# A decoder's recurrence on one core: TensorE's order written out over four head pairs, the triangular solve moved to GpSimd, and a plain fp32 start

## The chip, the cores and the metric

The kernel runs on one core of one Trainium2 chip. The metric is the device time of one execution in microseconds; lower is better. Three runs of the kernel before gave 2741.23, 2740.06 and 2737.32 us, so the time before is their median, 2740.06 us. A profiled execution gives the trace that is read below.

## The reference

The model is a trunk of two layers over 272 positions (16 meta tokens and 256 tokens) with 2048 channels: an RWKV-7 layer with a gated FFN, then a stick-breaking attention layer with another. The change touches only the first part, the RWKV-7 mixing and the norm ahead of it. Cut to what matters:

```python
hn = rms_norm(h, mix_norm_g[0])                     # over 2048 channels
xx = token_shift(hn) - hn
xr, xw, xk, xv, xa, xg = (hn + xx * mu[i] for i in range(6))
r, k, v = xr @ w_r, xk @ w_k, xv @ w_v              # 2048 x 2048 each
decay = exp(-exp(-softplus(-(dec_w0 + tanh(xw @ dec_w1) @ dec_w2)) - 0.5))
a = sigmoid(a_w0 + (xa @ a_w1) @ a_w2)
g = sigmoid(xg @ g_w1) @ g_w2
kk = normalise_per_head(k * k_k)                    # 32 heads of 64
k = k * (1 + (a - 1) * k_a)
# for every head, position by position:
sa = state @ -kk_t
state = state * d_t + outer(sa, kk_t * a_t) + outer(v_t, k_t)
y_t = state @ r_t
y = group_norm(y) * gn_w + gn_b
bonus = sum(r * k * r_k, per head) * v
h = h + ((y + bonus) * g) @ w_o
```

## The kernel before

Activations lie transposed: channels on the 128 partitions, 272 positions along the free dimension, 16 tiles for 2048 channels. A projection makes one block of 128 output channels from 16 k-tiles. To hold precision at speed, each weight tile and each activation is split into a high and a low part (ACT casts, DVE subtracts, L172/L173 for weights, L254/L255 for activations), and a k-tile is three matmuls (`mm3k`, L191 to L193). Weights come as raw tiles of 1024 columns, eight k-tiles, into three buffers (`raw`) over SyncE's queue, and the split parts go to six buffers of four k-tiles.

**Prologue** (L374 on). RMS norm, the shifted mixes, all 16 blocks of w_k, and the hidden layers of the small products dec_w1, a_w1 and g_w1. The first three w_k blocks are split ahead in `presplit` and run together, k-tile by k-tile, as the activations get ready; `key_out` adds each finished block's squares into the key norm `kq` (L469).

**Scan.** Sixteen pairs of heads; one call of the generator `pair` does one pair. The recurrence is computed in chunks: 16 meta positions, then four chunks of 64. In order of the code a pair goes through: LoRA products `zw`, `za` with their decay terms P and pe; the projections of v and r (32 k-tiles); score products `ba`, `bb`, masked into `G` (L721); the bonus sum (L727, `blk` in fp32) and `z0`; the triangular solve; `tb`, `tv`, `kv`; two doubling rounds `yb`, `zb` (the transpose `Tn`, L827, reads the solved blocks `Tt`); apply `wa` to `Ah`; trans `rm` to `Rh` and `Mp`; states and four steps into `cb` (L896, L903); group norm `vb` (L916), gate `gp`, and the output `o`.

The solve inverts 40 small triangles of 16 by 16. G and SC0 are written to DRAM (`s1`), read back with one triangle on each of 40 partitions (`As`), solved by one DVE instruction and 14 pairs of a multiply and an add (L772, L777, L779), written back (`s2`) and read into `Tt`. These transfers go by ACT's queue (L754, L756, L760, L780, L783).

`interleave` starts a pair every 13 ticks and advances all that run by a yield each; the scheduler then decides each engine's order. When all pairs have their fronts, `wo_head` begins the first four w_o blocks with 15 of 16 k-tiles, and `wo_first` finishes them and does the others.

After the scan come the first FFN, the attention and the second FFN, which the change leaves alone.

Of the kernel before, what the change touches and what calls it, by code (L numbers as in the profile page):

```python
# [40 lines left out]
L2B = {"da": 1, "g": 2}  # L41
# [3 lines left out]
NSQ = 4  # L45
RSTEP = 7
KR = 8
FRONT = {"zw", "za", "vc", "bonus", "ba", "bb", "z0", "k0", "b00", "b01"}
TAIL = {"wa", "rm0", "rm1", "cb", "vb", "gp"}
WAIT1 = 3  # L50
WAIT2 = 9
STRIDE = 13
PSTEP = 8
NHEAD = 4
KHEAD = 15
ASTRIDE = 2
ASTEP = 4
BUFS = {n: 2 for n in "ARV BK AR0 bv G An Tt pe X BV0 WV0".split()}


def _consts():
# [14 lines left out]
    put("blk", blk)  # L76
    put("blk64", blk / 64)
# [6 lines left out]
    put("mask3", np.concatenate([incl, strict, incl], 1))  # L84
# [20 lines left out]
    first = pos  # L105
    put("onesD", np.full((128, 128), 1.0 / D))
# [17 lines left out]
class Builder:  # L124
# [141 lines left out]
    def build(self):  # L266
        tc, nc = self.tc, self.nc
        with ExitStack() as ctx:
# [6 lines left out]
            nc.scalar.dma_start(self.vecs, self.a["vecs"])  # L275
            self.dvec = {"hdw0": 0, "ha0": NK, "oka": 2 * NK}
            self.dvec.update({f"om{i}": (3 + i) * NK for i in range(6)})
            self.dv = cp.tile([128, 9 * NK + 4], F32, name="dv")
            b = 9 * NK
            nc.vector.memset(self.dv[:, b:b + 1], RMS_EPS)  # L280
            nc.vector.memset(self.dv[:, b + 1:b + 2], GN_EPS)
            nc.vector.memset(self.dv[:, b + 2:b + 3], 1.0)
            self.eps = self.dv[:, b:b + 1]
            self.gneps = self.dv[:, b + 1:b + 2]
            self.one = self.dv[:, b + 2:b + 3]

            def v16(name):
                i = VEC.index(name) * NK
                return self.vecs[:, i:i + NK]

            for dst, src in (("hdw0", "dec_w0"), ("ha0", "a_w0")):
                o = self.dvec[dst]
                nc.vector.tensor_scalar(self.dv[:, o:o + NK], v16(src), 0.5, None, ALU.mult)
            nc.vector.tensor_scalar(self.dv[:, 2 * NK:3 * NK], v16("k_a"), -1.0, 1.0,
                                    ALU.mult, ALU.add)
            nc.vector.tensor_scalar(self.dv[:, 3 * NK:9 * NK], self.vecs[:, 0:6 * NK], -1.0, 1.0,
                                    ALU.mult, ALU.add)
            nv = len(VEC) * NK
            self.kgain = self.vecs[:, nv:nv + 1]
            self.qgain = self.dv[:, b + 3:b + 4]  # L300
            nc.vector.tensor_scalar(self.qgain, self.vecs[:, nv + 1:nv + 2], 128.0 ** -0.5, None,
                                    ALU.mult)
# [34 lines left out]

    def time_mix(self):
# [4 lines left out]
        self.xs2 = self.hid_ctx.enter_context(tc.tile_pool(name="xs2", bufs=2 * NK))  # L343
        self.kp = self.hid_ctx.enter_context(tc.tile_pool(name="kp", bufs=NK))
# [5 lines left out]
        self.fronts = 0  # L350
        with ExitStack() as ctx:
            sp = ctx.enter_context(tc.tile_pool(name="sp", bufs=1))
            self.l2 = ctx.enter_context(tc.tile_pool(name="l2", bufs=2))
            self.dq = nc.scalar
            self.static = []
            self.s2 = []
            zero = sp.tile([128, 5, 65], F32, name="zero", tag="P")
            nc.gpsimd.memset(zero, 0.0)
            for i in range(2):
                st = {}  # L360
                for n, w in (("B0", 64), ("V0", 64), ("SC0", 128)):
# [5 lines left out]
                                  zero.rearrange("p a t -> p (a t)"))  # L367
                self.s2.append(z)
            self.interleave(lambda p: self.pair(p, sp), STRIDE, self.wo_head())
# [4 lines left out]
    def prologue(self, hid):  # L374
# [3 lines left out]
        with ExitStack() as ctx:  # L378
# [3 lines left out]
            hn = [self.xs2.tile([128, T + 1], F32, name="hn", tag="s") for _ in range(NK)]  # L382
            xx = [self.xs2.tile([128, T], F32, name="xx", tag="s") for _ in range(NK)]
            for k in range(NK):
                nc.sync.dma_start(xx[k], a["xT"][:, k, :])
# [14 lines left out]
            rstd = self.rstd_of(ss[:, :T])  # L400


            w0 = [[] for _ in range(G0)]
            raws = []
            n = 0

            def presplit(k0):
                nonlocal raws, n
                if k0 % 8 == 0:
                    raws = []  # L410
                    for m in range(G0):
                        raw = self.wraw.tile([128, 1024], F32, name="raw", tag="raw")
                        nc.sync.dma_start(raw, a["w_k"][m][:, k0 * 128:k0 * 128 + 1024])
                        raws.append(raw)
                for m in range(G0):
                    pool, t = (wx, ("w", "w")) if n < NWX // 2 else (self.whl, ("whi", "wlo"))
                    hi = pool.tile([128, 512], F32R, name="whi", tag=t[0])
                    lo = pool.tile([128, 512], F32R, name="wlo", tag=t[1])
                    n += 1
                    part = raws[m][:, k0 % 8 * 128:k0 % 8 * 128 + 512]  # L420
                    A.copy(hi, part)
                    V.tensor_tensor(lo, part, hi.bitcast(F32), ALU.subtract)
                    for k in range(4):
                        w0[m].append((hi[:, k * 128:k * 128 + 128], lo[:, k * 128:k * 128 + 128]))
# [155 lines left out]
    def pair(self, p, sp):  # L580

        nc, a = self.nc, self.a
        V = nc.vector
# [612 lines left out]
```

## Time and profile before

| | us |
|---|---|
| median of three runs | 2740.06 |
| the profiled execution | 2741.77 |
| span of its trace | 2740.0 |
| first key sum (prologue's first three blocks done) | 53.4 |
| last key sum | 173.1 |
| first mask G of pair 0, last of pair 15 | 194.5, 629.7 |
| first sum of h after w_o | 686.5 |

So the prologue takes some 190 us, the scan some 490 us, and the three stages after it the other 2050 us. A row of the trace's timeline begins with start and duration in us, then engine, line, operation, destination<-source; a group's row ends with busy time, mean duration in ns and what the engine waited for just before. A bracket holds the idle time ahead of an instruction and what ended it. "PE" is TensorE, "PEld" its weight loads, "DVE" VectorE, "ACT" ScalarE, "POOL" GpSimd, "SP" SyncE, and a "q" behind the name its queue of DMA issues. The chain of waits is the chain of work that ended last, followed back.

### The profile page before, as it was taken

How to read it: one execution, taken by the hardware profiler on the slowest of the kernel's cores; microseconds unless marked ns; L12 is line 12 of the kernel's file. 1: busy time of each engine (PE TensorE's matmuls, PEld its weight loads, DVE VectorE, ACT ScalarE, POOL GpSimd, SP SyncE). 2: the span in 40 equal slices, each digit the busy share in tenths (PEclk: the TensorE clock that was granted, in tenths of full speed). 3: DMA queues.
4: the chain of work that ended last, by engine and by line, in shares of the span. 5: the costliest groups of instructions: out<-in, count | busy, mean ns of one | idle time of the engine just before them, and what ended most of it. 6: DMA issues, size and time to landing. Idle time of an engine off the chain costs nothing.

```text
span 2740.0 us, 53870 instructions
## 1 busy us (share of the span) xinstructions
PE 2689.3 (98%) x20862; PEld 2475.0 (90%) x20862; DVE 1864.8 (68%) x4176; ACT 1493.5 (55%) x3005; POOL 1.2 (0%) x11
## 2 busy tenths in 40 slices
PE   6999999998999999999999999999999999999999
PEld 5888888887999999999999999988888888888888
DVE  7677788786666555555556876577776666666665
ACT  6774555555554444444445764477555455454553
POOL 0000000000000000000000000000000000000000
PEclk9999999999999999999999999999999999999999
DMA  5443333332655555555555555533555665665655
GB/s 169 135 152 100 104 96 103 104 95 83 210 173 168 181 177 167 185 176 162 187 176 167 180 164 169 169 119 105 189 187 179 196 188 180 197 189 179 199 177 179
DMA packets 181279, 439.50 MB, mean 160 GB/s; under 512 B 57984, under 2 KB 84000, under 8 KB 181024
## 3 DMA queue, kind: packets, MB, share of 16 engines
q1 hardware_dynamic: 137632, 428.56, 49.4%
q10 hardware_dynamic: 43392, 7.52, 1.5%
q8 instruction: 163, 2.67, 0.4%
q14 instruction: 92, 0.75, 0.1%
HBM read 430.27 MB, written 5.74 MB: 159 GB/s over the span
## 4 chain that ended last, share of the span: by engine, by line
PE 91%; DVE 3%; DMA 3%; ACT 2%; ACTq 1%; issue 0%; SPq 0%; DVEq 0%
PE mm L197 22%; PE mm L191 16%; PE mm L193 16%; PE mm L192 15%; PE mm L196 11%; DMA raw<-w_k 1%; PE cb L903 1%; PE yb L831 1%; PE rm L871 1%; PE zb L848 1%; PE hms L1038 1%; PE cb L896 1%; PE z L1115 1%; DVE G L721 0%; PE ba L715 0%
## 5 line engine op out<-in xcount | busy, mean ns | idle before, releaser
L173 DVE TENSOR_TENSOR wlo<-raw,whi 128x512 fp32r<-128x512 f32 (+1 forms) x1596 | 1079.0, 679 | 622.3 <-ACT whi L172 598.7
L172 ACT CAST whi<-raw 128x512 fp32r<-128x512 f32 (+1 forms) x1596 | 967.6, 611 | 906.2 <-PE mm L192 577.0
L191 PE MATMUL mm<-hl,whi 128*128 128x272 f32 x3424 | 996.9, 292 | 19.4 <-ACT hl L254 18.5
L193 PE MATMUL mm<-hl,wlo 128*128 128x272 f32 x3424 | 995.9, 291 | 0.0
L192 PE MATMUL mm<-hl,whi 128*128 128x272 f32 x3424 | 991.4, 290 | 0.4 <-DVE hl L255 0.3
L197 PE MATMUL mm<-hl,whi 128*128 128x512 f32 x2624 | 919.8, 395 | 0.0
L196 PE MATMUL mm<-hl,wlo 128*128 128x256 f32 x2624 | 740.6, 282 | 0.0
L191 PEld LDWEIGHTS mm<-hl,whi 128*128 128x128 f32 x3424 | 645.8, 189 | 27.7 <-ACT hl L254 20.5
L192 PEld LDWEIGHTS mm<-hl,whi 128*128 128x128 f32 x3424 | 652.6, 191 | 4.2 <-DVE hl L255 1.3
L193 PEld LDWEIGHTS mm<-hl,wlo 128*128 128x128 f32 x3424 | 647.9, 189 | 4.8 <-issue 1.8
L197 PEld LDWEIGHTS mm<-hl,whi 128*128 128x128 f32 x2624 | 492.5, 188 | 112.7
L196 PEld LDWEIGHTS mm<-hl,wlo 128*128 128x128 f32 x2624 | 494.3, 188 | 0.6
L213 DVE TENSOR_TENSOR h<-h,mm 128x256 f32<-128x256 f32 (+1 forms) x224 | 93.9, 420 | 6.6 <-PE mm L197 6.0
L206 ACT COPY c<-mm 128x256 f32<-128x256 f32 x104 | 38.8, 373 | 79.0 <-PE mm L197 78.9
L191 PE MATMUL mm<-hi,whi 128*128 128x272 f32 x256 | 79.3, 310 | 0.0
L192 PE MATMUL mm<-lo,whi 128*128 128x272 f32 x256 | 77.0, 301 | 0.0
L193 PE MATMUL mm<-hi,wlo 128*128 128x272 f32 x256 | 76.6, 299 | 0.0
L193 PEld LDWEIGHTS mm<-hi,wlo 128*128 128x128 f32 x256 | 48.8, 191 | 2.9 <-issue 2.4
L191 PEld LDWEIGHTS mm<-hi,whi 128*128 128x128 f32 x256 | 48.9, 191 | 2.4
L192 PEld LDWEIGHTS mm<-lo,whi 128*128 128x128 f32 x256 | 48.9, 191 | 1.0
L428 ACT ACTIVATE u<-hn,vecs 128x272 f32<-128x272 f32 x96 | 45.2, 515 | 4.8 <-DVE hn L452 4.8
L1009 ACT ACTIVATE s<-t 128x272 f32<-128x272 f32 (+1 forms) x88 | 37.5, 426 | 18.6 <-DVE t L208 18.5
(275 smaller groups left out, 2158.6 us busy)
## 6 DMA issues: line engine op xcount, KB each, us to landing
raw<-w_gate SPq DMA_DIRECT2D x176, 512.0 KB
raw<-w_up SPq DMA_DIRECT2D x176, 512.0 KB
raw<-w_down SPq DMA_DIRECT2D x128, 512.0 KB
raw<-w_down SPq DMA_DIRECT2D x128, 192.0 KB
raw<-w_k SPq DMA_DIRECT2D x32, 512.0 KB
raw<-w_v SPq DMA_DIRECT2D x32, 512.0 KB
raw<-w_r SPq DMA_DIRECT2D x32, 512.0 KB
raw<-w_o SPq DMA_DIRECT2D x32, 512.0 KB
```

The costliest lines, as they stand in the source:

```text
L172: nc.scalar.copy(hi, part)
L173: nc.vector.tensor_tensor(lo, part, hi.bitcast(F32), ALU.subtract)
L191: mm(out, w[0], x[0], start=first, stop=False)
L192: mm(out, w[0], x[1], start=False, stop=False)
L193: mm(out, w[1], x[0], start=False, stop=last)
L196: mm(out[:, :n], w[1], x[0], start=first, stop=False, skip_group_check=True)
L197: mm(out, w[0], x[2], start=False, stop=last, skip_group_check=True)
L206: self.nc.scalar.copy(c, out[:, n:])
L213: self.nc.vector.tensor_tensor(h, h, out[:, c:c + n], ALU.add)
L428: A.mul(u, hn[k][:, :T], self.vec(f"mu{i}", k))
L831: PE.matmul(yb[r, i * 64:i * 64 + 64], An[r, i], Tt[r, i], start=True, stop=True)
L1009: nc.scalar.activation(s[:, :n], t[:, :n], AF.Silu)
```

## The change

**Scan.** The generator `pair` becomes a class `Pair` with a method for each step, and `scan` writes TensorE's order out by hand. Iteration n does the recurrence and the norm of pair n (A), the doubling rounds, apply and trans of n+1 (M), the scores, solve, tokens and values of n+2 (B) and the LoRA products of n+3 (C). `fill(k)` puts k-tiles of the next projections between them, 32 in an iteration. Only TensorE's order is fixed; the scheduler still orders the other engines. In core:

```diff
-            self.interleave(lambda p: self.pair(p, sp), STRIDE, self.wo_head())
+            with tc.manual_schedule(engines={mybir.EngineType.PE}):
+                self.scan(sp)
...
+        for n in range(-3, NK):
+            get = lambda i: pairs.get(n + i)
+            A, M, B, C = get(0), get(1), get(2), get(3)
+            f = fill if C else lambda k: fill(k / 2)
+            if A:
+                A.states()
+                A.step(1)
+            if B:
+                B.chunk0()
+            if A:
+                A.step(2)
+            if B:
+                B.scores(0)
+            if A:
+                A.step(3)
+            if B:
+                B.scores(1)
+            if A:
+                A.step(4)
+            if B:
+                B.neg()
+                B.bonus()
+            f(2)
+            if B:
+                B.tokens()
+            if C:
+                C.lora()
+            f(3 + (LEAD if n == -3 else 0))
+            if A:
+                A.norm()
+                f(1)
+                A.gate()
+                f(3)
+            else:
+                f(4)
+            if M:
+                M.left(16)
+            if B:
+                B.values()
+                B.solve()
+                if n + 2 == NK - 1:
+                    self.rot = self.rot[1:]
+            f(4)
+            for g in ("right", 16), ("left", 32), ("right", 32), ("apply", None), ("trans", None):
+                if M:
+                    getattr(M, g[0])(*g[1:] if g[1] else ())
+                f(3 if g[0] == "trans" else 4)
```

**Solver.** Its instructions go from DVE to GpSimd, its transfers from ACT's queue to SyncE's. GpSimd also gets the memsets of P and the copies of pe.

```diff
-            self.dq = nc.scalar
+            self.dq = nc.sync
...
+        b, V, As = self.b, self.nc.gpsimd, self.As
...
-        V.memset(P[:, 0:1], 1.0)
-        V.memset(Pc[:, :, 0:1], 1.0)
+        nc.gpsimd.memset(P[:, 0:1], 1.0)
+        nc.gpsimd.memset(Pc[:, :, 0:1], 1.0)
...
-        V.tensor_copy(pe[:, 0:1], P[:, 16:17])
-        V.tensor_copy(pe[:, 1:4], Pc[:, 0:3, 64])
+        nc.gpsimd.tensor_copy(pe[:, 0:1], P[:, 16:17])
+        nc.gpsimd.tensor_copy(pe[:, 1:4], Pc[:, 0:3, 64])
```

**Small products.** The bonus sum and the norm's sum multiply a split input with a block of ones (two split matmuls each). The product `vc`, which centred v, goes; `tv` becomes eight plain matmuls, four of them with the centring matrix. The norm's refinement is shorter, and gn_b moves into the last operation. w_o's head takes 12 k-tiles and `wo_first` the other four.

```diff
-        PE.matmul(bp[:, :T], self.cst("blk"), rs, start=True, stop=True)
+        bp = self.head_sums("bonus", self.b.blk[0], self.rk)
...
-        PE.matmul(vc[:, :T], self.cst("cen"), v, start=True, stop=True)
...
-                PE.transpose(tv[:, u:u + 128], x.rearrange("p s t -> p (s t)"), self.cst("ident"))
+                PE.matmul(tv[HS[r], u:u + 128], self.ARV[:, c, 1], b.cst("ident"), start=True, stop=True)
+                PE.matmul(tv[HS[1 - r], u:u + 128], self.ARV[:, c, 2], b.cst("cen"), start=True, stop=True)
...
-KHEAD = 15
+KHEAD = 12
```

**Prologue.** The first three w_k blocks and all of dec_w1, a_w1 and g_w1 (which was split) are plain fp32; `presplit` goes. The activations are loaded by two queues, the mixes of v come first, and the key norm is finished in two halves.

```diff
-                if k % 4 == 0:
-                    presplit(k)
...
-                xk.append(mix(2, k, x0))
+                x = xtile()
+                mixed(2, k, x)
                 for m in range(G0):
-                    self.mm3k(ps[m][:, :T], w0[m][k], xk[k], k == 0, k == NK - 1)
+                    o = k % 4 * 128
+                    nc.tensor.matmul(ps[m][:, :T], w0[m, k // 4][:, o:o + 128], x,
+                                     start=k == 0, stop=k == NK - 1)
+                xk.append(self.split(x, x0))
```

Where this moves instructions is seen on three engines, in a steady part of the scan. The number behind a name tells one tile from the next of the same name.

On TensorE, the recurrence of one pair before, from its states on (`cb`), with k-tiles of a projection (`mm`) inside it:

```order
L896 MATMUL cb<-G,X 64x64 x4
L903 MATMUL cb<-S,Mp 64x64 x2
L903 MATMUL cb<-Rh,S 64x64 x2
L191 MATMUL mm<-hi,whi 128x272
L192 MATMUL mm<-lo,whi 128x272
L193 MATMUL mm<-hi,wlo 128x272
L191 MATMUL mm<-hi,whi 128x272
L903 MATMUL cb<-S,Mp 64x64 x2
L903 MATMUL cb<-Rh,S 64x64 x2
L192 MATMUL mm<-lo,whi 128x272
```

The same place of the change, with the chunk product (`z`) and the scores (`ba`, `bb`) of the pair two behind:

```order
L1255 MATMUL cb<-S,Mp 64x64 x2
L1255 MATMUL cb<-Rh,S 64x64 x2
L1043 MATMUL z_3926<-AR_3591,B_0_2008 64x32 x2
L1046 MATMUL z_3926<-consts,B_0_2008 64x64 x2
L1048 MATMUL z_3926<-consts,V_0_2010 64x64 x2
L1255 MATMUL cb<-S,Mp 64x64 x2
L1255 MATMUL cb<-Rh,S 64x64 x2
L1063 MATMUL ba<-ARV,BK 128x128
L1063 MATMUL bb<-ARV,BK 128x128
L1063 MATMUL ba<-ARV,BK 128x128
L1063 MATMUL bb<-ARV,BK 128x128
L1255 MATMUL cb<-S,Mp 64x64 x2
```

The recurrence's steps stood between k-tiles; now only small products of another pair stand between them, and TensorE changes less often between the two kinds.

On DVE before, from the norm of one pair to the solver of the next: `Tn_5761` is the transpose of pair p, `Ts_6026` the solver of pair p+1, whose G was masked ahead of these rows:

```order
L928 TENSOR_TENSOR o_6036<-y_5975,gp_6029 128x272
L730 TENSOR_SCALAR bv_6007<-bv_6007,vecs_65 128x272
L827 STREAM_TRANSPOSE Tn_5761<-Tt_5664 128x256
L621 TENSOR_TENSOR dal_6134<-w2_6131,dah_6133 128x256
L173 TENSOR_TENSOR wlo_6358<-raw_6355,whi_6357 128x512
L836 TENSOR_TENSOR WV0_6063<-yb_6052,BV0_5562 128x64
```

In the change `Tn_5064` belongs to pair p, whose solver has just run on GpSimd, `Ah_4783` to pair p-1; the mask of pair p+1 stands 14 rows behind that transpose:

```order
L1194 TENSOR_TENSOR Tt_4193<-Tt_4193,zb_4748 128x256
L937 TENSOR_TENSOR gl_5039<-w2_5036,gh_5038 128x256
L168 TENSOR_TENSOR wlo_5058<-raw_5009,whi_5057 128x512
L1170 STREAM_TRANSPOSE Tn_5064<-Tt_4661 128x256
L1209 COPY Ah_4783<-wa_4774 128x256
L168 TENSOR_TENSOR wlo_5149<-raw_5146,whi_5148 128x512
L1032 TENSOR_TENSOR AR0_4527<-rs_4796,P_4509 128x16
L1033 TENSOR_TENSOR ARV_4525<-rs_4796,P_4509 128x4x64
L1225 TENSOR_TENSOR Mp_4816<-rm0_4817,consts_64 128x2x64
```

Before, Tn read a pair whose solve was long done, and came behind the next pair's G. Now Tn of the pair just solved comes ahead of the next G, and Ah and Mp of the pair before it stand behind Tn.

On SyncE in the change, one pair's cycle: raw weights and LoRA weights (`w2`) of later pairs, the solver's transfers, and the next weights:

```order
L156 DMA raw_5009<-w_v 128x1024
L1078 DMA s1_4427<-SC0_1_2020 64x64 x2
L1076 DMA s1_4427<-G_4424 64x4x64 x2
L1080 DMA As_4432<-s1_4427 40x16x16
L961 DMA rn_4960<-rkd_439 128x1x272
L1118 DMA s2_1_2022<-Ts_4629 40x16x16
L1121 DMA Tt_4661<-s2_1_2022 64x5x64 x2
L156 DMA raw_5146<-w_r 128x1024
L156 DMA raw_5207<-w_r 128x1024
L156 DMA raw_5274<-w_v 128x1024
L933 DMA w2_5422<-lora2 128x256
L933 DMA w2_5504<-lora2 128x256
```

SyncE's queue held only weights and rn in the scan before. Now it also waits for G, for s1, for the solver and for s2, with the next weights behind each wait. On GpSimd the copies of pe stand behind the solver's fourth and sixth step.

More of the change, by code (lines that the diff above doesn't have):

```diff
@@ L40 @@
 NWHL = 6
-L2B = {"da": 1, "g": 2}
 NRAW2 = 4
@@ L105, in _consts @@
     first = pos
+    put("blk", blk)
     put("onesD", np.full((128, 128), 1.0 / D))
@@ L399, in prologue @@
                 nc.tensor.matmul(ss[:, :T], od, acc, start=g == 0, stop=g == NK - 4)
[L400 to L424, printed above, removed]
+            ms = ss[:, :T]
+            r = self.rstd_p.tile([128, T], F32, name="rstd", tag="rstd")
+            rn = self.rstd_p.tile([128, T], F32, name="rstdt", tag="rstdt")
+            A.activation(r, ms, AF.Ln, bias=self.eps)
+            A.activation(r, r, AF.Exp, scale=-0.5)
+            V.tensor_tensor(rn, r, r, ALU.mult)
+            V.scalar_tensor_tensor(rn, ms, RMS_EPS, rn, ALU.add, ALU.mult)
+            V.scalar_tensor_tensor(rn, rn, -3.0, r, ALU.add, ALU.mult)
             def mixed(i, k, out):
```

916 lines of the change are left out of this document (494 added, 422 removed).

## The prediction

> **What bounds the kernel now.** I read the page's first two parts, then busy time by stretch, then the repeat of one instruction in the scan, then the waits.
>
> ```profile
> PE 2689.3 (98%) x20862; PEld 2475.0 (90%) x20862; DVE 1864.8 (68%) x4176; ACT 1493.5 (55%) x3005; POOL 1.2 (0%) x11
> ```
>
> TensorE is busy nearly all the time, and GpSimd (POOL) is free. The 98% is a mean over stages, so here are three stretches of 50 us (busy time of PE, its weight loads, DVE, ACT, POOL; then clock, DMA share, GB/s):
>
> ```profile
> 0.00:50.00 50.00, 28.11 (x144) 23.27 (x145) 35.99 (x104) 30.42 (x68) 0.20 (x4) 0.97 0.55 172
> 350.00:400.00 50.00, 49.17 (x588) 41.89 (x584) 40.45 (x154) 28.98 (x67) 0.00 (x0) 1.00 0.37 106
> 650.00:700.00 50.00, 42.52 (x386) 38.40 (x386) 27.13 (x60) 25.08 (x48) 0.00 (x0) 0.90 0.39 124
> ```
>
> There is idle TensorE time at the head (21.9 us of 50) and where the scan ends (7.5 us). In the middle of the scan TensorE is full, so a pair gets shorter there only if TensorE's own work gets shorter. How long a pair takes is the repeat of the score mask G:
>
> ```profile
> L721 DVE TENSOR_TENSOR G<-bb,consts x32: 408/415/425, 194.5 to 629.7; 128x256 f32<-128x256 f32 x32
> L721 DVE TENSOR_TENSOR G<-bb,consts x2: 414/420/425, 248.7 to 249.7; 128x256 f32<-128x256 f32 x2
> 394.05 0.42 DVE L721 TENSOR_TENSOR G<-bb,consts 128x256 f32<-128x256 f32 x1 [1.20 <-PE bb L715]
> 423.27 0.42 DVE L721 TENSOR_TENSOR G<-bb,consts 128x256 f32<-128x256 f32 x1 [1.20 <-PE bb L715]
> ```
>
> Pair 0 masks at 194.5, pair 2 at 248.7, and a steady pair takes 423.27 - 394.05 = 29.2 us.
>
> **The head.** Three w_k blocks lose their splits and run as plain fp32. The rows are a wait of the first 60 us, the removed DVE split in the stretch from 21 to 54 us, the first key sum, and a run of plain fp32 matmuls with the matmul behind it.
>
> ```profile
> PE mm L191 <- ACT hl L254: 12.1, 5, 6.7
> L422 DVE TENSOR_TENSOR wlo<-raw,whi 128x512 fp32r<-128x512 f32 x9 | 6.0, 682 | 0.0
> 53.43 1.35 PE L469 MATMUL kq<-s,consts 128*32 128x272 f32 x4
> 73.50 1.62 PE L497 MATMUL lr<-xi,raw 128*96 128x272 f32 x6
> 74.75 0.49 PE L191 MATMUL mm<-hl,whi 128*128 128x272 f32 x1
> ```
>
> TensorE waits 12.1 us here for activations that come through ACT and DVE. The change takes 12 splits of 0.682 us (8.2 us) out of DVE's way, and the matmul no longer waits for the activation's own split; I take -10 us for the first key sum, from 53.4 to about 43. Against it: six plain instructions take 74.75 - 73.50 = 1.25 us, so a k-tile costs 0.42 against 3 x 0.126 = 0.38 (spacing from the rows below). For g_w1's 32 k-tiles that is +1.3. The first LoRA weights now wait until the prologue's buffers are free, before which TensorE has little else: bounds 0 and 5.7 (the whole load in the row below), taken 3.7, nearer the load. **Head: -5.** If the projections turn out bound by arriving weights instead, it is +5.
>
> ```profile
> 173.69 5.66 DMA w<-lora
> ```
>
> **TensorE's work for a pair.** A small step inside the projection, then four runs from the chain of waits:
>
> ```profile
> 299.39 0.28 PE L191 MATMUL mm<-hi,whi 128*128 128x272 f32 x1
> 299.61 0.33 PE L903 MATMUL cb<-S,Mp 64*64 64x64 f32 x4
> 299.77 0.28 PE L903 MATMUL cb<-Rh,S 64*64 64x64 f32 x4
> 299.98 0.39 PE L192 MATMUL mm<-lo,whi 128*128 128x272 f32 x1
> 300.21 0.29 PE L193 MATMUL mm<-hi,wlo 128*128 128x272 f32 x1
> 300.34 0.29 PE L191 MATMUL mm<-hi,whi 128*128 128x272 f32 x1
> 294.07 0.66 PE vc L695 x2
> 294.72 1.22 PE rm L871 x16
> 297.62 0.96 PE cb L896 x28
> 304.92 0.53 PE vb L916 x2
> 321.23 0.59 PE tv L801 x4
> ```
>
> Split matmuls start 0.13 us apart (300.21 to 300.34). From 299.39 to 300.21 a step of eight small instructions costs 0.82 - 2 x 0.13 = 0.56 us, while inside a run eight take about 0.25; leaving the split kind and coming back costs 0.3 us. The written order has about 8 such visits a pair against about 14: -1.8. The vc product goes: -0.7. The two head sums become two split matmuls each, 0.25 instead of 0.53: -0.5. Eight plain products take the place of four transposes of 0.59: between 0 and twice that, taken +1.2, since their count doubles and they are plain fp32. Now the recurrence's steps stand with only scores between them, no k-tiles, so each waits for its eviction: 3 x 0.25 = +0.7 as an estimate, from the ends of neighbouring rows. Sum 29.2 - 1.1 = 28.1: with everything else hidden, a pair costs **28.1 us** of TensorE.
>
> **The loop that takes over.** Moving the solver shortens nothing by itself; DVE was not waited for at the end. But the order on DVE now has Tn, which waits for the solved pair, ahead of Ah of the pair before, and TensorE's fixed order makes the next G wait for that Ah. So G, transfers, solver, transfers, Tn, Ah, trans, states, steps, scores, G is a closed loop. Its solver rows:
>
> ```profile
> 273.05 0.20 DVE L777 TENSOR_TENSOR Tm<-Ts,As 40x44 f32<-40x44 f32 x1
> 273.28 0.20 DVE L779 TENSOR_TENSOR Ts<-Ts,Tm 40x44 f32<-40x44 f32 x1
> 0.27 0.10 POOL L1193 MEMSET const-float32-1.0<- 128x1 f32 x1
> 0.81 0.06 DVE L280 MEMSET dv<- 128x1 f32 x1 [0.81 <-PEq L1193]
> ```
>
> On DVE dependent steps stand 0.23 us apart when nothing is between. No row shows GpSimd doing a two-input operation. The nearest is the shortest memset: 0.10 against 0.06. Adding the difference gives 0.27 us a step; multiplying by the ratio gives 0.38; the low bound is the 0.20 that DVE's own instruction takes. I take **0.27**, because what differs in so small an instruction is its fixed part. Its transfers, and ACT's rows in the same stretch:
>
> ```profile
> 218.07 3.79 DMA s<-SC
> 258.05 3.40 DMA As<-s
> 275.92 3.21 DMA s<-Ts
> 425.49 0.60 ACTq L783 DMA_DIRECT2D Tt<-s  x1
> 429.90 0.44 DVE L827 STREAM_TRANSPOSE Tn<-Tt 128x256 f32<-128x256 f32 x1
> 422.83 0.49 ACT L918 ACTIVATE rs<-vb,dv 128x272 f32<-128x272 f32 x1
> 424.39 1.28 ACT L919 ACT_TABLE_LOAD   x1
> ```
>
> The four transfers are at most 3.8, 3.4, 3.2 and 4.4 (425.49 to 429.90), 14.8 us. These were with a busy ACT issuing them and weight loads under way. On SyncE's queue the weight loads behind a waiting transfer are held back, so the transfers run alone; I take three quarters, 3.0 + 2.2 + 2.4 + 3.4 = 11.0, as an estimate. What is queued behind them: two w_r and two w_v loads and two LoRA loads of later pairs. Three raw and six split buffers hold 48 k-tiles, one and a half pairs' worth, so they should cover the 17 us of SyncE's wait.
>
> The sum, from the first G: two masks 0.8, into As 5.2, so the solver starts at 6.0 and has done its first instruction and four steps at 7.6. Then a copy of pe on GpSimd waits for P, which ACT makes only after the norm's Ln: TensorE reaches vb after step, neg, bonus, five k-tiles, tokens and lora (6.3 by the rows above), then 0.5 + 1.3 + 0.2: 8.3. The other 24 steps at 0.27 and the two copies are done at 15.1, Tt is in at 20.9, and back to G it takes Tn 0.4, Ah 0.4, rm 1.2, its DVE results beside three k-tiles 1.1, states 1.2, three steps 1.4, chunk0 0.7, scores 1.5: 7.9. **Loop: 28.8 us**, so it decides over 28.1.
>
> **The sum**, against the profiled execution, 2741.8 us (span 2740.0 and 1.8 around it), which is 1.7 above the median of the runs. Head -5. From G of pair 0 to G of pair 2, 54.2 now: the first iteration has no steps and no apply (12 for its k-tiles and some 7 of small work), the second a full loop, 48: -6. Thirteen more pairs by 28.8 - 29.2: -5. The end of the scan holds these waits from 627 to 687 us:
>
> ```profile
> PE mm L191 <- ACT hl L254: 6.5, 2, 5.1
> ```
>
> TensorE waits 6.5 us there for the last splits; three more k-tiles of each w_o block are left for after the scan, which covers about half: -3. Together -19: 2722.6 in a profiled execution, **2721** at the median.
>
> **Rivals.**
> 1. *A slow GpSimd.* At 0.38 us a step, 24 steps behind the copy add 2.6: the loop is 31.4, thirteen pairs cost +28 and the kernel gives 2755. It decides from 0.33 us a step, where the loop is 30.3 and the head's gain is used up. For it speaks that nothing covers the loop any more, against it that 0.27 has 0.06 in hand. The rows also hold two worse forms. A step of twice DVE's 0.23 makes the loop 33.4 and the kernel 2781. And if GpSimd stood still whenever DVE reads two SBUF operands, it would lose time to this group, from two pairs' stretch (350 to 408 us), and to the smaller ones like it:
>
> ```profile
> L173 DVE TENSOR_TENSOR wlo<-raw,whi 128x512 fp32r<-128x512 f32 x16 | 10.9, 682 | 2.1 <-ACT whi L172 1.9
> ```
>
> That is 5.5 us a pair, and as much again for the elementwise group: some 38% of the loop, which stretches 6.5 us of steps to 10.5 and gives 2773. The Trainium skill states the first in "GPSIMD Engine Reference", section 3.1: an elementwise add of two inputs measured 1.96 times as long as on DVE; by it the time would be the 2781. It was at 2048 elements and these steps have at most 56, and the memset rows are between the two readings. The skill states the second in "SBUF — State Buffer", "Who interferes with whom": a DVE instruction with two SBUF inputs contends with a GpSimd one that reads SBUF; by it the time would be the 2773. GpSimd is idle in the scan of this trace, so nothing here bears it out or refutes it.
> 2. *SyncE's queue is no better.* With the four transfers at 14.8 the loop is 32.0 and the kernel 2762; it decides at about 13.2 us of transfers.
> 3. *The loop is hidden.* At 0.20 a step it is 27.1, TensorE's 28.1 decides, and the kernel gives 2712.
> 4. *It does not shorten a pair.* The loop merely takes TensorE's place at 29.2, and only head, start and end count: 2726.
>
> **How the numbers follow.** Forecast 0.30; rival 4 with its surroundings (loop 29.0 to 29.8) 0.20; rival 3 0.14; a loop of 29.8 to 30.7, which eats the rest, 0.11; rival 1 0.15, of which 0.04 is each worse form; rival 2 0.10. A measurement of this kernel tells 0.2%, 5.5 us, from no change. The first three are faster but for 0.03 of rival 4: 0.61. Within: 0.11 and some of the rest, 0.13. Slower: 0.26. The range runs from 2696 (rival 3 with the small costs of TensorE and head at their low ends, 16 us) to 2768 (rival 2 and the plain form of rival 1 with their margins); outside lie the two worse forms and small chances beyond.
>
> **What would show it.** First key sum near 43 us. G's repeat 28.8 us. GpSimd's steps 0.27 us apart, with one gap of about 0.7 at the copy of pe. PE's longest waits in the scan ahead of trans, for Ah. Wrong: steps over 0.33 us apart; PE waiting for split weights in the scan (SyncE's queue); a repeat of 28 with no wait at trans (rival 3).

## The result: 2822.8 us, and the profile after

Four runs of the changed kernel gave 2829.95, 2822.05, 2823.48 and 2819.80 us, a median of 2822.77; four of the kernel before 2739.38. The ratio is 1.0309, with a 95% interval of 1.0291 to 1.0327: **slower by 3.1%**, where 2721 was forecast. The profiled execution took 2829.95 us, 88.2 more than the profiled one before.

The page's first part, and two stretches of 50 us with the columns as before (busy PE, PEld, DVE, ACT, POOL; clock, DMA share, GB/s):

```profile
PE 2689.6 (95%) x20942; PEld 2487.1 (88%) x20942; DVE 1793.6 (63%) x3586; ACT 1488.7 (53%) x3005; POOL 190.1 (7%) x539
0.00:50.00 50.00, 29.86 (x104) 21.84 (x104) 31.89 (x98) 27.30 (x63) 0.20 (x4) 1.00 0.55 181
350.00:400.00 50.00, 39.77 (x507) 35.02 (x506) 27.09 (x68) 22.95 (x58) 11.68 (x35) 0.86 0.37 112
```

In the middle of the scan TensorE, full before (49.17 of 50), now stands still for 10.2 us of 50, its granted clock falls to 0.86, and no other engine has become the busy one: DVE, ACT and GpSimd are all under 28. That is the picture of a closed loop of waits, in which each engine waits for the next. The masks G of all pairs, pair 2's alone, and the first five sums of h after w_o (a run of four, then the fifth):

```profile
L1071 DVE TENSOR_TENSOR G<-bb,consts x16: 678/692/692, 203.1 to 709.7; 128x512 f32<-128x512 f32 x16
L1071 DVE TENSOR_TENSOR G<-ba,consts x16: 677/681/682, 203.7 to 710.3; 128x512 f32<-128x512 f32 x16
L1071 DVE TENSOR_TENSOR G<-bb,consts x1: 678/678/678, 255.6 to 255.6; 128x512 f32<-128x512 f32 x1
769.73 1.51 DVE L738 TENSOR_TENSOR h<-h,mm 128x272 f32<-128x272 f32 x4 [4.08 <-PE mm L188]
783.37 0.44 DVE L738 TENSOR_TENSOR h<-h,mm 128x272 f32<-128x272 f32 x1 [0.27 <-PE mm L188]
```

The first mask comes 8.6 us later than before. From it to the last mask take 507.2 us (203.1 to 710.3) against 435.2. From there to the fifth sum of h, the first behind the four blocks that w_o's head began, take 73.1 against 66.0 (before: 629.7 to 695.7). What follows, to the end of the span, is the same length (2828.1 - 783.4 = 2044.7, and 2740.0 - 695.7 = 2044.3). So of the 88, 72 lie between the first mask and the last, in the pairs themselves: a steady one takes (709.7 - 255.6) / 13 = **34.9 us** where 28.8 was forecast and 29.2 was before.

The waits of the stretch from 190 to 800 us (engine and line, what it waited for: total, times, longest):

```profile
DVE Tn L1170 <- DMA Tt<-s: 94.4, 16, 7.4
...
PE rm L1221 <- DVE Ah L1209: 62.5, 13, 6.3
```

TensorE waits 13 times, once in each steady pair, ahead of trans (`rm`) for Ah, and DVE waits for the solved blocks Tt at Tn, which stands in front of Ah. It is the loop that the prediction wrote down. One turn of it in the chain of waits (start, duration, what):

```profile
399.92 2.80 DMA s<-G
...
402.86 2.04 DMA As<-s
...
405.06 0.75 POOL Ts L1109
...
413.18 0.76 POOL Tm L1114
...
418.70 1.96 DMA s<-Ts
...
421.38 2.46 DMA Tt<-s
...
423.94 0.06 DVE Tn L1170
...
424.31 0.40 DVE Ah L1209
...
424.75 1.15 PE rm L1221 x16
425.90 0.52 PE mm L186
...
428.23 0.33 PE cb L1240 x4
...
432.63 1.27 DVE G L1071 x2
...
434.57 2.70 DMA s<-G
```

The same mask leaves for DRAM at 399.92 and at 434.57: a turn of 34.65 us. Cut at the same places as the prediction's sum, in us:

| piece of the turn | forecast | measured | from the rows |
|---|---|---|---|
| G to As | 5.2 | 5.1 | 399.92 to 405.06 |
| solver with its two copies | 9.1 | 13.6 | 405.06 to 418.70 |
| Ts to Tn | 5.8 | 5.2 | 418.70 to 423.94 |
| Tn to the next G | 7.9 | 8.7 | 423.94 to 432.63 |
| masks, until the transfer leaves | 0.8 | 1.9 | 432.63 to 434.57 |
| turn | 28.8 | 34.65 | |

Of the 5.9 us by which the turn was missed, 4.5 are the solver.

### The profile page after: what moved, and what is told of

It is laid out like the page before. It is cut to its first block, busy times and chain, and to the rows that moved or that the text cites. A ratio compares the mean times of both kernels' runs of the same rounds, so it can differ in the third digit from the quotient of the medians.

```text
span 2828.1 us, 54093 instructions
## 1 busy us (share of the span) xinstructions
PE 2689.6 (95%) x20942; PEld 2487.1 (88%) x20942; DVE 1793.6 (63%) x3586; ACT 1488.7 (53%) x3005; POOL 190.1 (7%) x539
## 4 chain that ended last, share of the span: by engine, by line
PE 81%; POOL 6%; DMA 5%; issue 4%; ACT 2%; DVE 1%; SPq 1%; ACTq 0%; DVEq 0%; POOLq 0%
PE mm L192 21%; PE mm L186 14%; PE mm L188 14%; PE mm L187 14%; PE mm L191 11%; POOL Ts L1116 3%; POOL Tm L1114 3%; DMA raw<-w_k 1%; PE lr L540 1%; DMA s<-Ts 1%; DMA Tt<-s 1%; DMA raw<-w_r 1%; PE hms L791 1%; ACT whi L167 1%; PE z L868 0%
## 5 line engine op out<-in xcount | busy, mean ns | idle before, releaser
L186 PE MATMUL mm<-hl,whi 128*128 128x272 f32 x3344 | 983.4, 294 | 4.2 <-ACT whi L167 2.5
L188 PE MATMUL mm<-hl,wlo 128*128 128x272 f32 x3344 | 975.0, 292 | 4.0 <-DVE wlo L168 4.0
L187 PE MATMUL mm<-hl,whi 128*128 128x272 f32 x3344 | 972.6, 291 | 0.0
L1114 POOL TENSOR_TENSOR Tm<-Ts,As 40x14 f32<-40x14 f32 (+6 forms) x224 | 80.0, 357 | 15.6
L1116 POOL TENSOR_TENSOR Ts<-Ts,Tm 40x14 f32<-40x14 f32 (+6 forms) x224 | 79.6, 355 | 17.6
L1221 PE MATMUL rm<-G,Ah 64*64 64x128 f32 x256 | 17.0, 403 | 62.5 <-DVE Ah L1209 62.5
L1211 ACT COPY X<-wa 64x256 f32<-64x256 f32 x32 | 11.7, 366 | 119.3 <-DVE Ah L1209 118.9
L1170 DVE STREAM_TRANSPOSE Tn<-Tt 128x256 f32<-128x256 f32 x32 | 14.1, 440 | 94.4 <-DMA Tt<-s 94.4
```

Of the source, the lines that this page charges most:

```text
L186: mm(out, w[0], x[0], start=first, stop=False)
L187: mm(out, w[0], x[1], start=False, stop=False)
L188: mm(out, w[1], x[0], start=False, stop=last)
L1114: V.tensor_tensor(t, Ts[:, 0:i, i:i + 1].to_broadcast([40, i, n]), As[:, i:i + 1, i + 1:].to_broadcast([40, i, n]), ALU.mult)
L1116: V.tensor_tensor(Ts[:, 0:i, i + 1:], Ts[:, 0:i, i + 1:], t, ALU.add)
```

## The experiments

Each row is a median of runs on one chip, and its ratio is to runs of the kernel before on the same chip. The rows stand on several chips: e1 to e4 on one, e5 to e8, e9 to e11 and e12 on three others; across them the ratios are to be compared, not the times. "Masks" is the time from the first mask G to the last in the profiled execution.

| run | edit | us | ratio to before (95%) | masks |
|---|---|---|---|---|
| before | | 2739.38 | | 435.2 |
| after | | 2822.77 | 1.0309 (1.0291 to 1.0327) | 507.2 |
| e1_tn_late | Tn behind the next G on DVE | 2836.73 | 1.0355 (1.0339 to 1.0370) | 517.7 |
| e9_wact_only | weights on ACT's queue | 2845.89 | 1.0390 (1.0376 to 1.0403) | 523.5 |
| e5_weights_act | both of these | 2730.29 | 0.9963 (0.9951 to 0.9975) | 407.8 |
| e2_dve_solver | solver on DVE | 2740.61 | 1.0002 (0.9993 to 1.0012) | 414.0 |
| e3_tn_late_dve | e1 and e2 | 2739.49 | 1.0002 (0.9993 to 1.0011) | |
| e4_wlo_memset | low parts of weights not computed | 2806.58 | a single run | 489.1 |
| e6_before_pool | kernel before, solver on GpSimd | 2841.03 | 1.0372 (1.0351 to 1.0394) | 536.5 |
| e7_head_only | kernel before, new prologue | 2739.97 | 1.0004 (0.9995 to 1.0013) | |
| e8_dve_oldhead | e2, old prologue | 2733.26 | 0.9970 (0.9960 to 0.9981) | |
| e10_wact_oldhead | e5, old prologue | 2727.12 | 0.9959 (0.9945 to 0.9972) | |
| e11_wact_oldhead_tail | e10, w_o's last k-tiles earlier | 2720.93 | 0.9934 (0.9922 to 0.9945) | 410.4 |
| e12_tail_dve | e11, solver on DVE | 2725.97 | 0.9945 (0.9932 to 0.9958) | 416.8 |

### Opening the loop at Tn: e1

Theory A: the loop exists only because Tn of pair p stands ahead of Ah of pair p-1 on DVE. Put Tn behind the next mask, and TensorE's own 28 us should decide.

```diff
-        V.transpose(self.Tn.rearrange(flat), Tt[:, :4].rearrange(flat))
+        if s == 16 and self.p + 1 < NK:
+            with b.tc.issue_after(b.pairs[self.p + 1].mask.ins):
+                V.transpose(self.Tn.rearrange(flat), Tt[:, :4].rearrange(flat))
```

> The changed kernel with one order edge added: on DVE the transpose Tn of pair p goes behind the mask G of pair p+1, so that it no longer stands ahead of Ah of pair p-1. Solver still on GpSimd, transfers still on SyncE's queue. Theory A (the scan is bound by the closed loop G, transfers, solver, transfers, Tn, Ah, trans, states, G, now 34.7 us): the loop is open, TensorE decides again, G repeats every 28 to 29.5 us, PE's wait for Ah (62.5 us in all) is gone, the kernel takes 2740 to 2755 us. Rival B (GpSimd's work slows DVE and with it everything): the repeat stays over 33 us and the time over 2800. Rival C (weights queued on SyncE behind the solver's transfers): 30 to 32 us, and PE waits for split weights, 2765 to 2790.

It came out 0.5% slower than the change itself. The chain of waits of this run, one turn:

```profile
410.42 0.61 SPq L1121
411.09 4.33 DMA raw<-w_r
415.44 0.63 ACT whi L167
416.09 0.69 DVE wlo L168
...
417.21 0.20 DVE Mp L1229
...
422.72 1.28 DVE G L1071 x2
...
424.66 3.10 DMA s<-G
427.91 2.05 DMA As<-s
...
430.11 0.81 POOL Ts L1109
```

A second loop decides now, and it runs through SyncE's queue. SyncE issues the load of Tt (L1121) only when the solved blocks are out. The raw w_r that stands behind it leaves at 411.09, ACT casts it, DVE subtracts it, and behind that subtraction on DVE stands Mp, without which TensorE's steps and the next scores can't run. Then G goes to the solver again. A steady pair takes 36.2 us, (716.4 - 246.1) / 13 from its masks. Theory A alone was wrong: one loop was opened and another of about the same length stood behind it. The time is one that rival B named, but the chain shows rival C's queue, at a higher price than C had; e5 below tells the two apart.

### The solver back on DVE: e2 and e3

```diff
-        b, V, As = self.b, self.nc.gpsimd, self.As
+        b, V, As = self.b, self.nc.vector, self.As
```

> The changed kernel with the solver's 29 instructions back on DVE (transfers stay on SyncE's queue). The scheduler then puts Tn behind the next G by itself, so two things are undone at once. Theory A: repeat 28 to 29.5 us, 2735 to 2755 us. Theory of an equally slow scan (the fixed order of TensorE costs more by itself than the old one): the repeat stays over 30 us.

> Solver on DVE and Tn of pair p forced behind G of pair p+1. Against e2 nothing should change if the scheduler had already put Tn there (within 0.3%); against e1 it tells what the solver's engine costs once the loop is open: by theory A nothing (within 0.5%), since the solver is off the path on either engine; by rival C e3 is faster than e1 by 2 us a pair, 25 us or more.

Both give back the whole loss, and nothing more: the kernel without the solver's move is as fast as the kernel before. A steady pair takes 27.7 us (masks of pairs 2 and 15 at 255.0 and 615.4), so the pairs gain 21 us on the kernel before. The rest of the kernel takes it away again: the first mask comes 6.9 us later, and from the last mask to the fifth sum of h pass 77.6 us against 66.0. In e2 the scheduler itself put Tn behind the next G, so e2 and e3 hardly differ. Nor do they show a faster solver. One solve of e2, first and last instruction, and SyncE's queue meanwhile:

```profile
405.72 0.41 DVE L1109 TENSOR_TENSOR Ts<-As,consts 40x256 f32<-40x256 f32 x1
...
420.51 0.18 DVE L1116 TENSOR_TENSOR Ts<-Ts,Tm 40x14 f32<-40x14 f32 x1
```

```profile
414.47 4.66 SPq L156 DMA_DIRECT2D raw<-w_v  x2
...
420.71 0.30 SPq L1118 DMA_DIRECT2D s<-Ts  x1
```

Spread over DVE's other work, the solve takes 15.0 us here (405.72 to 420.69), more than the 13.6 on GpSimd. But the raw weights are issued ahead of the store of Ts, where in the change they stood behind it. So with the solver's engine the scheduler changed both orders. That fits e3, which is 97 us faster than e1 where theory A allowed 0.5%: Tn is forced to the same place in both, but in e3 too the raw weights are issued ahead of the store of Ts (409.23 and 414.29, and 420.54). Neither e2 nor e3 tells GpSimd's slowness from the order. That is what e5 is for.

### Opening both loops, the solver still on GpSimd: e5 and e9

Scan weights go to ACT's queue, with (e5) and without (e9) e1's order of Tn.

```diff
-            nc.sync.dma_start(raw, src[:, j0 * m:j1 * m])
+            (nc.scalar if getattr(self, "inscan", False) else nc.sync).dma_start(raw, src[:, j0 * m:j1 * m])
```

> e1 (solver on GpSimd, Tn behind the next G) with the streamed raw weights of the scan issued on ACT's queue, so that SyncE's holds only the solver's transfers, rn and the LoRA weights. In e1 G still repeats every 36 us and the chain runs G, s1, As, solver, s2, Tt's issue, raw w_r behind it, its split on ACT and DVE, the scores, G: theory C (the second loop closes through SyncE's queue). Theory C: both loops are open now, G repeats every 28 to 30 us, the kernel takes 2738 to 2765 us although the solver's steps stay at 0.44 us. Rival B (a slow solver on GpSimd holds the scan in any order, through DVE's port or P and pe): repeat over 33 us, over 2800. In between (ACT's own waits delay the loads): 30 to 33 us.

> The changed kernel with the scan's raw weights on ACT's queue and nothing else; Tn of pair p still stands ahead of Ah of pair p-1 on DVE. It parts the two loops. Two loops (the prediction's through Tn, and the one through SyncE's queue): the first is still closed, G repeats every 33 to 35 us, 2795 to 2825 us. If the queue alone was the cause: 28 us and 2730 to 2740.

Each edit alone leaves the kernel slower than the change (e1, e9); together they bring it below the kernel before, some 3.4% under the change by the ratios, and 8 us under the range that theory C gave. In e9 TensorE still waits 13 times ahead of `rm` for Ah, 81.2 us in all, so the first loop is still closed there. It lies 21 us above its expected range; in one turn of it the store of Ts takes 3.55 us where the change's took 1.96, at a DMA share of 0.66 against 0.21, but whether that is the reason in every turn was not followed. The masks and the middle of the scan in e5:

```profile
L1073 DVE TENSOR_TENSOR G<-ba,consts x16: 678/680/684, 201.3 to 609.1; 128x512 f32<-128x512 f32 x16
350.00:400.00 50.00, 47.70 (x660) 42.54 (x658) 34.69 (x91) 32.34 (x80) 19.54 (x58) 1.00 0.39 109
```

TensorE is busy for 47.7 of 50 us at a full clock, and a steady pair takes 27.7 us, as with the solver on DVE (pair 2's mask at 248.8, pair 15's at 608.5). In e5 the waits from 260 to 640 us hold no wait of TensorE for Ah any more. GpSimd's steps have not become faster: the multiplies take 385 ns on the mean, against 357 in the change. So the time that the solver takes on GpSimd is not lost as such. It is lost only as long as a loop of waits is closed over it.

### What a solver step costs: e4

In the scan, DVE's subtraction for the streamed weights becomes a memset of the low part (the low parts of w_v, w_r and the first w_o blocks are left out of the computation), which reads no SBUF.

```diff
-                nc.vector.tensor_tensor(lo, part, hi.bitcast(F32), ALU.subtract)
+                if getattr(self, "inscan", False):
+                    nc.vector.memset(lo.bitcast(F32), 0.0)
```

> The changed kernel, but in the scan DVE writes zeros to the low part of the streamed weights instead of subtracting (the low parts of w_v, w_r and the w_o head are left out of the result). DVE then has 0.68 us less of two-operand work from SBUF for each split, nothing else changes. Theory L (GpSimd's steps stand still while DVE reads two operands from SBUF): steps 0.44 us apart on the mean come down to 0.34 to 0.37, G's repeat from 34.7 to about 32. Rival (a step on GpSimd just takes that long): steps stay at 0.42 to 0.45 and the repeat stays within 0.7 us.

The expectation was met in part. The solver's multiplies as groups, first of the kernel before (on DVE), then of the change, then of e4 (busy time, mean ns | idle time ahead of them):

```profile
L777 DVE TENSOR_TENSOR Tm<-Ts,As 40x14 f32<-40x14 f32 (+6 forms) x224 | 42.0, 188 | 2.3
L1114 POOL TENSOR_TENSOR Tm<-Ts,As 40x14 f32<-40x14 f32 (+6 forms) x224 | 80.0, 357 | 15.6
L1119 POOL TENSOR_TENSOR Tm<-Ts,As 40x14 f32<-40x14 f32 (+6 forms) x224 | 71.7, 320 | 15.6
```

The mean fell from 357 to 320 ns, and a steady pair from 34.9 to 33.9 us, (687.6 - 246.6) / 13 from its masks. The same steps, apart by what DVE did meanwhile, from the timeline of the change (first GpSimd, then DVE):

```profile
412.81 0.29 POOL L1116 TENSOR_TENSOR Ts<-Ts,Tm 40x56 f32<-40x56 f32 x1
413.18 0.75 POOL L1114 TENSOR_TENSOR Tm<-Ts,As 40x54 f32<-40x54 f32 x1
414.01 0.62 POOL L1116 TENSOR_TENSOR Ts<-Ts,Tm 40x54 f32<-40x54 f32 x1
```

```profile
412.76 0.42 DVE L1179 TENSOR_TENSOR Ys<-yb,consts 128x256 f32<-128x256 f32 x1 [0.17 <-PE yb L1177]
413.10 1.38 DVE L168 TENSOR_TENSOR wlo<-raw,whi 128x512 fp32r<-128x512 f32 x2
```

The multiply of 40x54 that runs beside two subtractions of weights, both of whose operands lie in SBUF, takes 0.75 us; a 40x56 add beside a product whose one input is the matmul result `yb` takes 0.29. Over all 406 neighbouring steps of the change, start to start, by what DVE ran between them:

| DVE between the two starts | steps | mean us |
|---|---|---|
| nothing | 80 | 0.311 |
| only work without two SBUF operands | 41 | 0.351 |
| two SBUF operands for over half of the time | 249 | 0.509 |
| all | 406 | 0.443 |

The 36 steps that the table leaves out met such work for a shorter time. In e4 the mean over all is 0.396, with 0.325 when DVE does nothing, and 182 steps instead of 285 met any two-operand work. What is left in e4 would be the elementwise group of the pair, which was not taken out. So a step costs 0.31 undisturbed and some 0.2 more under such DVE work; e4, a single run, confirms the direction with the weights' part, not the whole of it.

### The move alone, in the kernel before: e6

The 29 solver instructions of the kernel before go to GpSimd, all else stays.

```diff
-        V.tensor_tensor(Ts.rearrange("p i t -> p (i t)"), As.rearrange("p i t -> p (i t)"),
+        nc.gpsimd.tensor_tensor(Ts.rearrange("p i t -> p (i t)"), As.rearrange("p i t -> p (i t)"),
...
-            V.tensor_tensor(t, Ts[:, 0:i, i:i + 1].to_broadcast([40, i, n]),
+            nc.gpsimd.tensor_tensor(t, Ts[:, 0:i, i:i + 1].to_broadcast([40, i, n]),
...
-            V.tensor_tensor(Ts[:, 0:i, i + 1:], Ts[:, 0:i, i + 1:], t, ALU.add)
+            nc.gpsimd.tensor_tensor(Ts[:, 0:i, i + 1:], Ts[:, 0:i, i + 1:], t, ALU.add)
```

> The kernel before with one edit: the solver's 29 instructions on GpSimd, everything else as it was (transfers on ACT's queue, the generator's order). In the kernel before the solver is spread over some 13.6 us of DVE (408.3 to 421.9) and Tn stands behind the next pair's G; on GpSimd it takes some 13 us. Theory A/C (the solver costs only where a loop closes over it): within 1% of before, 2735 to 2765 us. Rival B (the move itself costs 5 us a pair): 2800 us or more.

This is 76 us above the range of theories A and C, and in the range of rival B, which has the move itself cost 5 us a pair. In the old kernel Tn stands behind the next G, yet a loop closes there too, over ACT, whose queue carries the solver's transfers. Waits of this run from 260 to 700 us, and ACT's timeline:

```profile
ACT whi L172 <- POOL Ts L779: 59.4, 12, 5.9
...
PE vc L695 <- ACT v L661: 44.9, 12, 4.7
```

```profile
421.26 0.28 ACTq L780 DMA_DIRECT2D s<-Ts  x1
421.58 0.62 ACT L172 CAST whi<-raw 128x512 fp32r<-128x512 f32 x1 [4.79 <-POOL Ts L779]
422.10 0.38 ACT L661 COPY v<-mm 128x272 f32<-128x272 f32 x1
```

ACT stands at the issue of `s<-Ts` for 4.79 us until GpSimd is done, and the cast and the copy of v that TensorE waits for stand behind that issue. So the two kernels close different loops over the same slower solver; for e6 that is read from the waits, and no edit tested it. That the move costs this by itself, as rival B has it, does not fit e5, where a steady pair loses nothing by it. The waits are not the whole price either: from the first mask to the last TensorE is busy for 469.60 us instead of 423.92 with the same work, at a mean granted clock of 0.91 instead of 0.99.

### Head and end: e7, e8, e10, e11, e12

e7 is the kernel before with the prologue's part of the change alone; e8 and e10 are e2 and e5 with that part taken back. Its core, as e7 has it:

```diff
-                if k % 4 == 0:
-                    presplit(k)
...
-                    self.mm3k(ps[m][:, :T], w0[m][k], xk[k], k == 0, k == NK - 1)
+                    nc.tensor.matmul(ps[m][:, :T], w0[m, k // 4][:, o:o + 128], x,
+                                     start=k == 0, stop=k == NK - 1)
```

> The kernel before with the changed prologue alone (three w_k blocks, dec_w1, a_w1 and g_w1 in plain fp32, activations over two queues, key norm in halves); scan as before. By the trace of the change G of pair 0 is 7 to 9 us later than before and nothing is gained behind it: 2744 to 2750 us, G of pair 0 at 201 to 204 us. By the prediction's term (head -5): 2734 us.

> e2 (solver on DVE, the rest of the new scan) with the prologue of the kernel before. If the new prologue costs 7 us and the new scan is otherwise the same, 2731 to 2735 us, faster than before by 0.2 to 0.3%. If the head's delay is absorbed by the scan, 2738 to 2742 us.

> e5 (solver on GpSimd, both loops open) with the prologue of the kernel before. e2 to e8 gained 7 us by the old prologue, but the new one cost the old scan nothing (e7). If the new scan starts its first pairs as soon as the prologue lets it, 2722 to 2726 us; if its start is bound otherwise, 2728 to 2732.

The new prologue changes nothing in the old kernel: e7 neither loses what its expectation read from the trace (2744 to 2750 us) nor gains the prediction's 5. With the new scan and the solver on DVE the old prologue is faster by 0.3%, and the intervals of e2 and e8 lie apart; with e5's scan the difference of e10 lies inside them. The first mask comes at 196.8 in e8 against 201.4 in e2, and at 198.5 in e10 against 201.3 in e5. Why the new prologue costs something in one scan and nothing in the other stays open.

e11 moves w_o's last four k-tiles of the first four blocks from `wo_first` to right behind the scan, ahead of the closing of the scan's buffers:

```diff
+        w = [self.weights(a["w_o"][m][:, KHEAD * 128:], NK - KHEAD, 128) for m in range(NHEAD)]
+        for k in range(KHEAD, NK):
+            for m in range(NHEAD):
+                self.mm3k(self.wo[m], w[m][k - KHEAD], self.o[k], False, k == NK - 1)
         self.hid_ctx.close()
```

> e10 with the last four k-tiles of the first four w_o blocks taken right behind the scan, inside the scan's weight pools, so that their loads can run while the last pairs finish; in the change they wait until the scan's pools are closed. From G of pair 15 to the fifth sum of h it takes 77 us in e2 and e5 against 66 before. If the late loads (6.3 and 5.0 us in e2's chain of waits) are the cause, 6 to 11 us less than e10: 2712 to 2719. If the drain of a pipeline four pairs deep is, within 2 us of e10.

e12 is e11 with e2's edit.

> e11 with the solver's 29 instructions on DVE, all else as in e11 (weights on ACT's queue, Tn late, old prologue, early tail). With the loops open the solver is on no path: if its engine then does not matter, within 3 us of e11's 2720.9. If freeing DVE of 5.6 us a pair is worth something, e12 is slower by 5 us or more; if GpSimd's two-operand work slows DVE, e12 is faster by 3 us or more.

The end of the scan in the chain of waits, first e2, then e11:

```profile
666.16 6.29 DMA raw<-w_o
...
673.85 5.00 DMA raw<-w_o
```

```profile
660.96 4.47 DMA raw<-w_o
```

With the four k-tiles left for `wo_first`, two loads of w_o stand one after the other on the path, 11.3 us; with them pulled forward, one of 4.5. Against e10, on the same chip, e11 is 6.2 us faster by the medians, with intervals that just touch; from the last mask to the fifth sum of h pass 66.8 us instead of 75.7. e11 is the fastest version: 2720.93 us, **0.9934 of the kernel before (0.9922 to 0.9945)**, with the solver on GpSimd. e12, the same with the solver on DVE, is 5 us behind by the medians, but it ran on another chip and the two intervals overlap. Its end takes 73.6 us though it has e11's edit, so the two loads are not all that makes the end long. Whether GpSimd is the better place once the loops are open was not settled.

## Why the prediction was wrong

**The step that failed** is the loop's sum, in its solver term: "I take 0.27, because what differs in so small an instruction is its fixed part". The steps came 0.443 us apart on the mean, and the solver took 13.6 us instead of 9.1. Neither bound held it (0.20 and 0.38), since I bounded the step by a memset, which reads nothing, while these steps read two operands beside a DVE that does the same. The price splits into 0.08 a step for a slower engine (0.31 undisturbed against DVE's 0.23) and 0.13 on the mean for DVE's work beside it.

**The rival that came nearest** was the first, a slow GpSimd, in its worse forms, with 0.04 each. The form with a step of twice DVE's, 0.46, had the solver's price right: 24 steps x 0.19 more is 4.6 us a pair, and 4.5 came. That the two agree so well is in part luck: in the turn above the first instruction and four steps took 2.1 instead of 1.6, and the wait of 0.7 for P at the copy of pe, which the sum held, did not come (GpSimd waits there in 3 of 16 pairs). "GPSIMD Engine Reference", section 3.1, of the Trainium skill has an add of 2048 elements at 1.96 times DVE's time, and here the multiplies' mean durations, 357 against 188 ns, stand at 1.90. But the mechanism is not that one alone: undisturbed the steps stand at 0.31 / 0.23 = 1.35, and the rest is the second form, DVE's work beside them, as the step at 413.18 shows, 0.75 us beside two subtractions. "SBUF — State Buffer", "Who interferes with whom", of the Trainium skill has a DVE instruction with two SBUF inputs contend with a GpSimd one that reads SBUF; the trace agrees, 0.509 against 0.311 us a step. The form of twice DVE's step gave 2781 and the time is 42 above it: 1.5 us a pair more (20 in 13 pairs), and head, start and end, which were forecast at -14 and came at +14, less what the profiled execution took beyond the median. The range ended at 2768 and left both forms out.

**The loop itself** was right: its members, the place where TensorE waits (ahead of trans, for Ah, 13 times), and that GpSimd would be in it. So was its transfer term: 10.4 us in the turn above against 11.0. The piece from Tn to G was short by 0.8: its three k-tiles took 2.33 us (425.90 to 428.23) against 1.1 and the states 1.4 against 1.2, while steps, chunk0 and scores came at 3.0 against 3.6. What the k-tiles' term had not priced is the clock. TensorE has idled before `rm`, and the stretch right behind it shows:

```profile
424.00:428.00 4.00, 3.25 (x25) 2.84 (x25) 1.57 (x5) 2.24 (x5) 0.00 (x0) 0.50 0.95 346
```

The granted clock is 0.50, and the split matmuls start 0.23 us apart instead of 0.13. `rm` takes 1.15 us, and in e2, at a granted clock of 1.00,

```profile
655.89 0.61 PE rm L1221 x16
```

The sum had `rm` at 1.2, from a row of the kernel before, so its term came out right by luck. From 260 to 700 us the granted clock is 0.90 on the mean; in e2 it is 1.00 from 260 to 600. In this loop TensorE's waits made its own pieces longer. The masks' term was short by 1.1: two masks of 128x512 take 1.27, not 0.8, and behind them SyncE needs 0.6 (433.93 to 434.53) to issue the first of G's two transfers, ahead of the one that the chain follows.

**SyncE's queue** was wrong: "Three raw and six split buffers hold 48 k-tiles ... so they should cover the 17 us of SyncE's wait". In the change itself this is hidden behind the first loop; e1 shows that the first load behind Tt's decides as soon as that loop is opened. The prediction had seen a single loop where there were two.

**TensorE's 28.1 us** a pair came close: 27.7 in e2 and e5, where TensorE is busy for over 324 of the 340 us from 260 to 600. Its single terms were not measured. A hidden loop, as in rival 3, is what e5 shows, but by two other orders and not by a faster step.

**The head** was wrong: -5 forecast, +8.6 measured at the first mask. The first key sum came at 51.4, not near 43:

```profile
24.41 24.76 PE L470 MATMUL mm<-xi,raw 128*128 128x272 f32 x96 [4.24 <-DVE xi L432]
51.37 0.65 PE L488 MATMUL kq<-xi,consts 128*32 128x272 f32 x2
```

I had asked when the splits get out of DVE's way, and not when the first activation is there (24.41) nor how long 48 plain k-tiles then take: 24.76 us, 0.52 each instead of 0.42, to 49.2. The row that gave 0.42 has 96 output channels, and these have 128; whether that is the difference was not tested. The other case that the prediction named, arriving weights, was there before already. Two links of the chain of waits of the kernel before, ahead of its first key sum:

```profile
25.07 6.91 DMA raw<-w_k
...
41.15 7.15 DMA raw<-w_k
```

The prediction read the waits there, which named activations, and not the chain, which holds the loads. Yet e7 shows no loss from this prologue by itself (its first mask is at 195.2), so the +8.6 is not explained by it alone, and the rest of its cause stays open.

**The start and the end**: from pair 0's mask to pair 2's took 52.5 (203.1 to 255.6) instead of 54.2, -1.7 where -6 was forecast: the first iteration took 19.7, as its 12 and 7 had it, but the full loop behind it 32.8. The end was taken at -3 and gave +7.1; e11 shows a cause, the k-tiles left for later, whose weights weren't loaded until the scan was over, and e12 that it is not the only one.

With the measured terms: 8.6 - 1.7 + 13 x (34.9 - 29.2) + 7.1 = 88, which is the difference.

## What to carry to other kernels

When an order is written out by hand, look for closed loops: follow an instruction's result through every queue, DMA issue queues and in-order engines too, until it comes back to the same instruction of the next round. A slower engine in such a loop costs its whole delay each round, and here it cost a steady pair nothing once the loops were open; there may be a second loop behind the first, so one edit that does nothing is no proof against it. Price an engine by a row with its neighbour at work, and where no row has that, keep the price beside a busy neighbour in the range.

## What was not expected of the hardware

- GpSimd's steps of 14 to 56 elements stood 0.31 us apart beside an idle DVE, only 0.08 more than DVE's own, and one of 54 elements took 0.75 us beside DVE subtractions of 128x512 with two SBUF operands.
- Where TensorE waited up to 6.3 us in each turn of the loop, its granted clock was 0.50 in the 4 us behind the wait, and a run of 16 matmuls (`rm`) took 1.15 us, against 0.61 in e2 at a clock of 1.00.
